# Layer 1 of a two-layer diffusion trunk on one core: inputs of the recurrences projected first, values projected per head and transposed

## The chip, the cores and the metric

The kernel runs on one core of a Trainium2 chip. Its time is the device time of one execution in microseconds; the time of a kernel is the median of several executions. Engines are named as in the profile: PE (TensorE, matrix products), DVE (VectorE), ACT (ScalarE), POOL (GpSimd), SP (SyncE, whose queue issues nearly all transfers here).

## The reference, cut to what matters

Two layers over 1024 latent and 256 context tokens of 1024 channels; each is a mixer and a SwiGLU FFN. Layer 1's mixer is a bidirectional chunked GLA of four heads beside a bidirectional RG-LRU of 512 channels:

```python
def project(h):
    q, k, v, g, lr, zg, zx = jnp.split(h @ w_in, ODD_SPLITS, axis=-1)
    ...
    logit = jnp.einsum('btnr,nrk->btnk', lr, gate_w) + gate_b
    log_a = jax.nn.log_sigmoid(logit) / GLA_GATE_NORM          # per head and direction
    xr = centred_conv(zx, conv_w, conv_b)                       # four taps
    return q, k, v, log_a, g, zg, xr
...
for d in range(2):                                              # forward and backward
    oc, S_ctx = gla_chunked(f(qc), f(kc), f(vc), f(lac[:, :, d]), S0)
    ol, _ = gla_chunked(f(ql), f(kl), f(vl), f(lal[:, :, d]), S_ctx)
    ac, uc = rglru_coeffs(f(xrc), wa[d], ba[d], wx[d], bx[d], lam[d])
    hcd = linear_scan(ac, uc, h0)                               # h = a * h + u, token by token
    al, ul = rglru_coeffs(f(xrl), wa[d], ba[d], wx[d], bx[d], lam[d])
    hld = linear_scan(al, ul, hcd[:, -1])
...
y_gla = rms_norm(o_gla, gla_g).reshape(B, T, -1) * jax.nn.silu(g)
y_lru = h_lru * jax.nn.gelu(zg)
return jnp.concatenate([y_gla, y_lru], axis=-1) @ w_out
```

## The kernel before

Tokens lie in three chunks `CH`: 256 of context, 512 and 512 latent. Activations are kept with channels on the partitions. A product of full precision is made from three of reduced precision: weight and activation are each split into a high and a low part, and `mm3` adds high x high, low x high and high x low over 8 slices of the 1024 channels, so one projection of 128 output channels costs 24 products for each token chunk. `wload` brings a weight piece of 128 output channels (512 KB), copies the high part on ACT and subtracts for the low part on POOL.

Layer 1 begins with `kq` of heads 0 to 2 (at the end of `layer0`), then `layer1`: `proj_lr` (the gates' low rank part); then, woven one step against one, `gla_gates` (for each head three products into the one PSUM bank of tag `d`, a log-sigmoid on DVE, ACT and POOL, a store `dz` to HBM) and `proj1v` (values of all four heads for 128 tokens at a time: the tokens are the stationary operand and 512 value columns move, so that tokens come out on the partitions as the GLA wants them; its weights are split by `v1_load`). Then `kq` of head 3, and the list `LO`, which names single-letter steps with a part or head number m:

- x: `proj_zx`, inputs of the RG-LRU, part m of four, stored to HBM as `dzx`;
- z: `proj_zg`, its gelu gate, a chain of DVE and ACT steps from PSUM on tile `gt`, stored as `dzg`;
- l: `lru`, the recurrence of part m: `zx` loaded back, the four-tap convolution `xr` on DVE, twelve gate products `lg`, their tanh on ACT (`tr`, `ti`), then for both directions exponentials, square roots and the scans (`lq`) on ACT, POOL and DVE;
- p: `gla_prep` of head m in three token chunks: loads of `kq` and `dz`, running sums (`pc`) by scans on DVE, exponentials on ACT, products (`pb`, `pk`, `qh`) on POOL and DVE, stores. Every tile of it has one buffer;
- g: `proj_g`, the GLA's output gate (`stg`).

After the list come the GLA's heads: `gla_states` transposes the stored keys (`kt`), and `gla_half` loads `kq`, `V`, `C`, makes differences `D` on POOL, their exponential on ACT, and products `kx`, `qx` on DVE for the intra-chunk matrices.

Projections and `lg` take their PSUM banks in turn from seven (`BANKS`). A scheduler fixes the order of each engine's instructions when the kernel is built; each engine, and SP's queue of transfers, then runs strictly in that order. Tiles in SBUF and banks in PSUM are reused when their last reader is done.

Of the kernel before, what the change touches and what calls it, by code (L numbers as in the profile page):

```python
# [46 lines left out]
ZA, ZB, ZL = 1, 1, 0  # L47
VQ = (0, 2)
# [74 lines left out]

def weave(a, b, na, nb=1, lead=0):

    live = [True, True]

    def step(i, gen, n):
        for _ in range(n):
            if live[i] and next(gen, run) is run:  # L130
                live[i] = False

    step(0, a, lead)
    while any(live):
# [4 lines left out]
class Trunk:
# [1373 lines left out]
    def v1_load(self, pool):  # L1513
        nc, a = self.nc, self.a
        vh = pool.tile([P, KT, 512], F32R, name="v1h")
        vl = pool.tile([P, KT, 512], F32R, name="v1l")
        for q in range(4):
            raw = self.wraw(a["w1v"][q], f"v1_{q}")
            raw = raw.rearrange("p (k c) -> p k c", k=2)
            nc.scalar.activation(vh[:, 2 * q:2 * q + 2], raw, AF.Copy)  # L1520
            (nc.vector if q in VQ else nc.gpsimd).tensor_tensor(vl[:, 2 * q:2 * q + 2], raw, vh[:, 2 * q:2 * q + 2].bitcast(F32), op=ALU.subtract)
        return vh, vl
# [154 lines left out]
    def layer1(self, h, h2x, l1):  # L1677
# [21 lines left out]
        w = self.wload(a["w1"][3], "w1_3")  # L1699
        for ci in range(3):  # L1700
            self.kq_chunk(w, h[ci], 3, ci, pp, "pk", 1)
        for op, m in LO:
            if op == "x":
                self.proj_zx(h, lp, m)
            elif op == "z":
                self.proj_zg(h, lp, m)
            elif op == "g":
                self.proj_g(h, lp, m)
            elif op == "p":
                self.gla_prep(pp, m)  # L1710
            else:
                self.lru(lp, m)
# [209 lines left out]
def prep(i):  # L1922
# [84 lines left out]
```

## Time and profile before

| | us |
|---|---|
| median of 3 executions (3209.05 to 3218.72) | 3209.83 |
| profiled execution, device time | 3204.12 |
| its span from first to last instruction | 3201.9 |
| PE busy, of the span | 2921.8 (91%) |
| DVE busy | 2186.1 (68%) |
| ACT busy | 1266.0 (40%) |
| POOL busy | 1268.2 (40%) |

The profile shows one execution: for each engine which instruction ran when, and for idle time which event ended it. Matrix products are pipelined, so a busy PE is not one at its peak: pace is read from the distance of starts. The clock granted to TensorE is a share of full speed, where 1.00 is 2.4 GHz and 0.50 is 1.2 GHz.

### The profile page before, as it was taken

The numbers are of one execution on the slowest core, as the hardware profiler recorded it, in microseconds if no ns is written. First come the engines' busy times: TensorE is split into PE (matmuls) and PEld (weight loads), VectorE is DVE, ScalarE is ACT, GpSimd is POOL, SyncE is SP. The second block draws the span as 40 slices with busy tenths as digits, with TensorE's granted clock in tenths as the row PEclk, the third lists the DMA queues.
The fourth block names the chain that finished last, engine by engine and source line by source line (L and its number), as shares of the span: only waits on it lengthen the run. The fifth ranks groups of instructions, "written<-read, shape, count | busy, mean of one in ns | idle before, by whom it ended". The sixth has DMA issues, their size and how long they took to land. (4 is left out here: it accounts for less than half of the span.)

```text
span 3201.9 us, 40796 instructions
## 1 busy us (share of the span) xinstructions
PE 2921.8 (91%) x14848; PEld 2380.8 (74%) x14848; DVE 2186.1 (68%) x3700; ACT 1266.0 (40%) x1956; POOL 1268.2 (40%) x745
## 2 busy tenths in 40 slices
PE   7998899988979999999989998866888999999988
PEld 4987677766768888888877777645677777778877
DVE  5598878885686555556688517879867675645487
ACT  4311655653442232324453444463333332333343
POOL 2333423332233233234445224454545444333445
PEclk9999899998989999999999999987999999999998
DMA  6576433315425444447423235465323232233452
GB/s 250 173 239 204 113 90 88 99 31 188 156 81 162 145 152 152 145 151 273 154 83 112 93 105 187 155 204 187 105 87 99 79 100 93 95 104 104 151 177 98
DMA packets 214920, 437.49 MB, mean 137 GB/s; under 512 B 23424, under 2 KB 86656, under 8 KB 214464
## 3 DMA queue, kind: packets, MB, share of 16 engines
q1 hardware_dynamic: 210112, 418.12, 40.2%
q10 hardware_dynamic: 4608, 16.78, 1.7%
q8 instruction: 116, 1.90, 0.2%
q14 instruction: 84, 0.69, 0.1%
HBM read 325.11 MB, written 109.71 MB: 136 GB/s over the span
## 5 line engine op out<-in xcount | busy, mean ns | idle before, releaser
L263 DVE SCALAR_TENSOR_TENSOR adaw<-adaw,cr 128x1024 f32<-128x1024 f32 x96 | 139.2, 1450 | 88.2 <-DMA adaw<-adat 88.1
L758 POOL TENSOR_TENSOR l_fx<-r_fin,h_fx 128x1024 fp32r<-128x1024 f32 x36 | 87.8, 2439 | 266.5 <-ACT h_fx L757 266.5
L758 POOL TENSOR_TENSOR l_fw<-r_fin,h_fw 128x1024 fp32r<-128x1024 f32 x36 | 87.1, 2420 | 167.4 <-ACT h_fw L757 147.6
L537 POOL TENSOR_SCALAR s_d<-s_d,cf_d 128x1280 f32<-128x1280 f32 (+1 forms) x40 | 46.6, 1165 | 255.4 <-DVE nb_d L524 97.2
L517 PE MATMUL ps_d<-kd,q 128*128 128x512 f32 (+1 forms) x416 | 119.9, 392 | 16.1 <-DVE s_d L519 12.4
L519 DVE TENSOR_SCALAR_CACHE_REDUCE s_d<-ps_d 128x512 f32<-128x512 f32 (+1 forms) x208 | 116.8, 581 | 12.9 <-PE ps_d L517 11.9
L870 DVE TENSOR_TENSOR r_fin<-r_fin,r_fin 128x512 f32<-128x512 f32 x36 | 24.9, 691 | 135.8 <-POOL l_fx L758 135.5
L363 PE MATMUL pq<-hhi,h_w 128*128 128x512 f32 (+1 forms) x312 | 113.4, 363 | 2.6 <-DVE yl L434 2.6
L363 PE MATMUL pq<-hlo,h_w 128*128 128x512 f32 (+1 forms) x312 | 111.6, 358 | 0.0
L363 PE MATMUL pq<-hhi,l_w 128*128 128x512 f32 (+1 forms) x312 | 111.5, 357 | 0.0
L530 ACT ACTIVATE s_d<-s_d,nb_d 128x1280 f32<-128x1280 f32 (+1 forms) x80 | 94.6, 1184 | 23.8 <-DVE nb_d L525 21.5
L538 POOL TENSOR_TENSOR s_d<-s_d,s_d 128x1280 f32<-128x1280 f32 (+1 forms) x40 | 99.6, 2491 | 3.3
L1630 PE MATMUL pg<-qx,kx 128*128 128x128 f32 x448 | 70.8, 308 | 32.8 <-DVE qx L1626 30.1
L956 POOL TENSOR_TENSOR bl<-r_b,bh 128x1024 fp32r<-128x1024 f32 (+2 forms) x32 | 65.4, 2052 | 85.0 <-ACT bh L955 82.3
L1630 PEld LDWEIGHTS pg<-qx,kx 128*128 128x128 f32 x448 | 63.3, 216 | 43.4 <-issue 21.1
L431 POOL TENSOR_TENSOR rsh<-rsh,rope 128x512 f32<-128x512 f32 x26 | 40.7, 1567 | 135.4 <-DVE rsh L428 96.3
L517 PEld LDWEIGHTS ps_d<-kd,q 128*128 128x128 f32 x416 | 70.4, 198 | 31.8 <-DVE s_d L519 18.1
L956 POOL TENSOR_TENSOR bl_0t<-r_b0t,bh_0t 128x1024 fp32r<-128x1024 f32 (+1 forms) x24 | 67.4, 2815 | 62.3 <-ACT bh_0t L955 62.3
L363 PE MATMUL pd<-bh,h_fo 128*128 128x512 f32 (+1 forms) x228 | 85.8, 378 | 5.4 <-DVE xz L1012 3.0
L1620 POOL TENSOR_TENSOR D<-C,V 128x256 f32<-128x256 f32 x56 | 49.1, 876 | 103.0 <-DVE qx L1626 91.8
L327 DVE TENSOR_TENSOR nacc<-nacc,nsq 128x512 f32<-128x512 f32 (+1 forms) x77 | 75.9, 989 | 19.1 <-ACT nsq L326 16.9
L1622 ACT ACTIVATE D<-D 128x512 f32<-128x512 f32 x56 | 35.3, 630 | 134.5 <-POOL D L1621 134.5
(629 smaller groups left out, 10447.6 us busy)
## 6 DMA issues: line engine op xcount, KB each, us to landing
r_fin<-fin SPq DMA_DIRECT2D x104, 512.0 KB, 3.6
adaw<-adat SPq DMA_DIRECT2D x64, 512.0 KB, 3.7
q<-dq SPq DMA_DIRECT2D x160, 128.0 KB, 3.0
adaw<-adat ACTq DMA_DIRECT2D x32, 512.0 KB, 4.5
r_wo<-wo SPq DMA_DIRECT2D x32, 512.0 KB, 3.8
w<-fo SPq DMA_DIRECT2D x32, 512.0 KB, 6.8
r_w<-w SPq DMA_DIRECT2D x29, 512.0 KB, 4.1
dbt<-et SPq DMA_DIRECT2D x44, 256.0 KB, 2.4
```

Source lines behind the costliest of these rows:

```text
L263: nc.vector.scalar_tensor_tensor(o, w, 1.0, cs[v], op0=ALU.mult, op1=ALU.mult, accum_out=self.adac[l][:, m, v:v + 1])
L327: nc.vector.tensor_tensor(acc, acc, sq, op=ALU.add)
L363: nc.tensor.matmul(out, w[wi][wsl(k)], x[xi][xsl(k)], start=(first and k == 0 and i == 0), stop=(last and k == nk - 1 and i == 2), skip_gr ...
L517: nc.tensor.matmul(pt[:, 0:kn], q[:, m, ab, j * P:(j + 1) * P], kt[:, m, k0:k0 + kn], start=(ab == 0), stop=(ab == 1))
L519: nc.vector.tensor_scalar(s[m][:, k0:k0 + kn], pt[:, 0:kn], 1.0, None, op0=ALU.mult, op1=ALU.max, accum_out=mx[:, m, c:c + 1])
L530: nc.scalar.activation(s[m][:, 0:nk * P], s[m][:, 0:nk * P], AF.Exp, bias=nb[:, m:m + 1], scale=SC, accum_out=sm[:, m:m + 1])
L537: nc.gpsimd.tensor_scalar(a1, a1, cf, 0.0, op0=ALU.mult, op1=ALU.add)
L538: nc.gpsimd.tensor_tensor(a0, a0, a1, op=ALU.add)
L758: eng.tensor_tensor(lo[:, 0:n], raw[:, 0:n], hi[:, 0:n].bitcast(F32), op=ALU.subtract)
L956: eng.tensor_tensor(lo[:, 0:n], raw, hi[:, 0:n].bitcast(F32), op=ALU.subtract)
L1620: nc.gpsimd.tensor_tensor(w4(d)[:, :, 0], r, w4(v)[:, :, 0], op=ALU.subtract)
L1630: nc.tensor.matmul(pg[:, b], kx[:, b], qx[:, b], start=True, stop=True)
```

## The change

Layer 1's list is cut in two. `LA1` holds the inputs and gates of recurrences 0 and 1, the recurrences themselves and the values of heads 0 and 1, and is woven with the gates; `LO` holds the rest. Values are projected like every other part, with a weight piece per head as the stationary operand and the tokens moving; the result has channels on the partitions, is copied to SBUF by ACT, transposed in blocks of 128 by PE into the bank of tag `d`, copied again and stored. The pieces are new columns 16 to 19 of `w1`. `pz` and `pe` of the gates have one buffer instead of two. `kq` of head 3 becomes step k of the second list.

```diff
-ZA, ZB, ZL = 1, 1, 0
-VQ = (0, 2)
+ZA, ZB, ZL = 2, 1, 0
...
-LO = [(o[0], int(o[1])) for o in "x0 x1 z0 l0 z1 p0 x2 g0 l1 p1 x3 z2 g1 l2 z3 p2 g2 g3 p3 l3".split()]
+ops = lambda text: [(o[0], int(o[1])) for o in text.split()]
+
+LA1 = ops("x0 z0 x1 l0 v0 z1 l1 v1")
+LO = ops("x2 z2 l2 k3 p0 x3 z3 v2 l3 p1 v3 p2 g0 p3 g1 g2 g3")
...
-            z = pool.tile([P, NTOK], F32, tag="pz", bufs=2, name=f"pz{m}")
-            e = pool.tile([P, NTOK], F32, tag="pe", bufs=2, name=f"pe{m}")
+            z = pool.tile([P, NTOK], F32, tag="pz", bufs=1, name=f"pz{m}")
+            e = pool.tile([P, NTOK], F32, tag="pe", bufs=1, name=f"pe{m}")
...
-    def proj1v(self, h, pool, v):
...
-                pv = self.psum(f"pv1_{tt}", BANKS)
-                self.mm3(pv, [x[:, :, j * P:(j + 1) * P] for x in h[ci]], v, KT,
-                         lambda k: (slice(None), k), lambda k: (slice(None), k))
-                st = pool.tile([P, 512], F32, tag="st", bufs=3, name=f"stv{tt}")
-                self.evac(st, pv, tt)
-                nc.sync.dma_start(self.dv[:, tt, :], st)
+    def proj_v(self, h, pool, m):
+
+        nc = self.nc
+        for ci, pt in self.proj(16 + m, h, (0, 1, 2), "pv"):
+            c0, cn = CH[ci]
+            t0, nt = c0 // P, cn // P
+            f = pool.tile([P, 512], F32, tag="st", bufs=4, name=f"vf{m}{ci}")
+            nc.scalar.activation(f[:, 0:cn], pt, AF.Copy)
+            pv = self.psum(f"vt{m}{ci}", "d")
+            for j in range(nt):
+                nc.tensor.transpose(pv[:, j * P:(j + 1) * P], f[:, j * P:(j + 1) * P], self.ident)
+            st = pool.tile([P, 512], F32, tag="st", bufs=4, name=f"stv{m}{ci}")
+            self.evac(st[:, 0:cn], pv[:, 0:cn], ci)
+            nc.sync.dma_start(self.dv[:, t0:t0 + nt, m * P:(m + 1) * P], st[:, 0:cn].rearrange("p (t c) -> p t c", c=P))
...
-            with self.pool("v1") as vp, self.pool("vs") as vs, self.pool("pg") as pp:
-                v = self.v1_load(vp)
-                weave(self.gla_gates(pp), self.proj1v(h, vs, v), ZA, ZB, ZL)
...
+        with self.pool("pg") as pg:
+            weave(self.gla_gates(pg), stages(LA1, None), ZA, ZB, ZL)
         pp = l1.enter_context(self.pool("pp"))
...
+        run(stages(LO, pp))
```

What this makes of the order is shown at three places. First PE at the first recurrence, before: the last product of gate `zg8_2` (part 0's second latent chunk), then the group `lg` (the digits after the part number are direction, gate and first token).

```order
L363 MATMUL zg8_2_17296<-h227_16346,h_w1_8_17260 128x512
L1388 MATMUL lg0000_17349<-xr0_17336,r_lg0_17345 128x256
L1388 MATMUL lg000256_17352<-xr0_17336,r_lg0_17345 128x512
L1388 MATMUL lg000768_17355<-xr0_17336,r_lg0_17345 128x512
L1388 MATMUL lg0010_17358<-xr0_17336,r_lg0_17345 128x256
L1388 MATMUL lg001256_17361<-xr0_17336,r_lg0_17345 128x512
L1388 MATMUL lg001768_17364<-xr0_17336,r_lg0_17345 128x512
L1388 MATMUL lg0100_17379<-xr0_17336,r_lg0_17345 128x256
```

And now: the last product of the inputs of part 1, and gate products `lz` of GLA head 2 inside the group.

```order
L365 MATMUL zx13_2_16863<-h227_16346,h_w1_13_16803 128x512
L1434 MATMUL lz2_0_16893<-lrt_16531,gw_16532 128x256
L1390 MATMUL lg0000_16922<-xr0_16909,r_lg0_16918 128x256
L1390 MATMUL lg000256_16925<-xr0_16909,r_lg0_16918 128x512
L1390 MATMUL lg000768_16928<-xr0_16909,r_lg0_16918 128x512
L1390 MATMUL lg0010_16931<-xr0_16909,r_lg0_16918 128x256
L1390 MATMUL lg001256_16934<-xr0_16909,r_lg0_16918 128x512
L1434 MATMUL lz2_256_16897<-lrt_16531,gw_16532 128x512
L1390 MATMUL lg001768_16937<-xr0_16909,r_lg0_16918 128x512
L1390 MATMUL lg0100_16952<-xr0_16909,r_lg0_16918 128x256
```

The group has moved from behind the gates of part 0 to behind the inputs of part 1, beside the GLA gates. Second the DVE at the end of the last recurrence (part 3, `lq30` forward and `lq31` backward), before:

```order
L1491 SCALAR_TENSOR_TENSOR stg31_18430<-stg31_18430,g7_1_18405 128x512
L1491 SCALAR_TENSOR_TENSOR stg32_18459<-stg32_18459,g7_2_18434 128x512
L1399 SCALAR_TENSOR_TENSOR ti30_18563<-ti30_18563,xr3_18551 128x1280
L1397 SCALAR_TENSOR_TENSOR lq30_18583<-lq30_18583,tr30_18562 128x1280
L1400 TENSOR_TENSOR ti30_18563<-ti30_18563,lq30_18583 128x1280
L1402 SCALAR_TENSOR_TENSOR lq30_18583<-av30_18582,ti30_18563 128x1280
L1397 SCALAR_TENSOR_TENSOR lq31_18613<-lq31_18613,tr31_18592 128x1280
L1626 TENSOR_TENSOR kx0_18667<-kq00_18742,D000_18762 64x4x64
L1626 TENSOR_TENSOR kx0_18667<-qk00_18744,D000_18762 64x4x64
L1399 SCALAR_TENSOR_TENSOR ti31_18593<-ti31_18593,xr3_18551 128x1280
```

And now, where `stv` are the copies of transposed values, `pc`, `pz` belong to `gla_prep` (two digits: head and chunk) and `stg` to the output gates:

```order
L1402 TENSOR_TENSOR ti31_18117<-ti31_18117,lq31_18137 128x1280
L1407 SCALAR_TENSOR_TENSOR lq31_18137<-av31_18136,ti31_18117 128x256
L1408 SCALAR_TENSOR_TENSOR lq31_18137<-av31_18136,lq31_18137,ti31_18117 128x1024
L1482 TENSOR_TENSOR pc12_18207<-pqk12_18202,pf12_18208 64x512
L1483 TENSOR_TENSOR pc12_18207<-pkq12_18201,pb12_18219 64x512
L1411 SCALAR_TENSOR_TENSOR lq31_18137<-lq31_18137,gl3_18073 128x1024
L1309 COPY stv30_18266<-vt30_18263 128x256
L1462 SCALAR_TENSOR_TENSOR pc20_18345<-ones_71,pz20_18344 128x128 x2
L1465 TENSOR_TENSOR pz20_18344<-pc20_18345,pz20_18344 64x256
L1309 COPY stv32_18336<-vt32_18331 128x512
```

Before, the recurrence ends among the GLA's first steps (`kx`, `qx`); now it ends ahead of the values of head 3 and of `gla_prep` of heads 2 and 3. Third SP's queue of transfers at the hand-over to the GLA's first head (names ending in 00 and `kh0`, `vs0`, `lvm` are its loads), before:

```order
L1477 DMA dkt3_16497<-pk32_18536 128x512
L1492 DMA dsg2_16471<-stg22_18395 128x512
L1482 DMA dqh3_16493<-pc32_18520 128x512
L1372 DMA gl3_18549<-dzg3_16506 128x1024
L189 DMA r_wo1131_19460<-wo1 128x1024
L1492 DMA dsg3_16472<-stg31_18430 128x512
L1556 DMA kh0_18661<-dkt0_16494 128x1280
L1492 DMA dsg3_16472<-stg32_18459 128x512
L1558 DMA vs0_18663<-dv_16481 128x10x128
L1543 DMA lvm_18665<-lvm 128x896
L1596 DMA kq00_18742<-dkq0_16105 128x512
```

And now:

```order
L1459 DMA pz32_18539<-dz3_16604 128x512
L1494 DMA dsg3_16472<-stg32_18751 128x512
L1534 DMA lvm_18795<-lvm 128x896
L1587 DMA kq00_18872<-dkq0_16105 128x512
L1467 DMA dc3_16485<-pc32_18540 128x512
L1468 DMA dvv3_16489<-pz32_18539 128x512
L1592 DMA qk00_18874<-dkq0_16105 64x512
L1479 DMA dkt3_16497<-pk32_18556 128x512
L1593 DMA qk00_18874<-dkq0_16105 64x512
L1484 DMA dqh3_16493<-pc32_18540 128x512
L1587 DMA V00_18877<-dvv0_16486 128x512
L1587 DMA C00_18879<-dc0_16482 128x512
```

The GLA's loads of `V` and `C` stood behind the last store of `gla_prep` by way of output gates; now they stand right behind it, and `lvm` and `kq00` wait ahead of it for the end of the projections.

## Rows read from the trace of the kernel before

**Rows 1.** Busy us (instructions) by stretch: PE, PEld, DVE, ACT, POOL, clock, DMA, GB/s
```profile
1840.00:1908.00 68.00, 68.00 (x274) 48.84 (x274) 11.21 (x17) 28.76 (x32) 18.36 (x7) 1.00 0.33 115
1908.00:2090.00 182.00, 159.64 (x664) 119.92 (x663) 124.66 (x131) 89.11 (x132) 81.39 (x57) 0.92 0.52 167
2090.00:2161.00 71.00, 46.62 (x173) 33.45 (x172) 57.23 (x48) 40.89 (x54) 40.26 (x29) 0.84 0.62 197
2161.00:2320.00 159.00, 119.24 (x658) 98.89 (x657) 142.53 (x269) 56.81 (x86) 84.50 (x81) 0.85 0.46 147
```

**Rows 2.** Timeline of DVE: start, us, engine, line, out<-in, size, xcount [idle before <-releaser]
```profile
2010.52 1.21 DVE L1409 SCALAR_TENSOR_TENSOR lq<-lq,gl 128x1024 f32<-128x1024 f32 x1
...
2160.90 0.84 DVE L1626 TENSOR_TENSOR kx<-kq,D 64x256 f32<-64x256 f32 x1
...
2162.23 1.49 DVE L1399 SCALAR_TENSOR_TENSOR ti<-ti,xr 128x1280 f32<-128x1280 f32 x1
...
2172.45 1.22 DVE L1409 SCALAR_TENSOR_TENSOR lq<-lq,gl 128x1024 f32<-128x1024 f32 x1 [1.66 <-POOL lq L1408]
```

**Rows 3.** Timeline of PE: recurrence groups lg, with projections between
```profile
1960.16 3.60 PE L1388 MATMUL lg<-xr,r_lg 128*128 128x256 f32 x10
...
1973.93 6.72 PE L1388 MATMUL lg<-xr,r_lg 128*128 128x256 f32 x12 [5.65 <-DVE gt L1359]
...
1980.09 0.79 PE L363 MATMUL zg<-h,h_w 128*128 128x512 f32 x1
...
2062.34 0.39 PE L363 MATMUL g<-h,h_w 128*128 128x512 f32 x1
...
2073.23 0.59 PE L1388 MATMUL lg<-xr,r_lg 128*128 128x256 f32 x2
...
2074.70 2.64 PE L1388 MATMUL lg<-xr,r_lg 128*128 128x512 f32 x6 [0.88 <-DVE xr L1378]
...
2090.23 0.79 PE L363 MATMUL zg<-h,h_w 128*128 128x512 f32 x1
...
2137.11 1.19 PE L1388 MATMUL lg<-xr,r_lg 128*128 128x256 f32 x2 [13.65 <-issue]
```

**Rows 4.** Timeline of PE: eight transposes of the GLA
```profile
2277.59 1.04 PE L1566 MATMUL kt<-ident,kh 128*128 128x128 f32 x8
```

**Rows 5.** Timeline of DVE: zx of part 0 copied, and back from HBM
```profile
1941.14 0.67 DVE L1307 COPY stx<-zx 128x512 f32<-128x512 f32 x1
...
1950.54 0.82 DVE L1376 TENSOR_SCALAR xr<-zx,lp 128x1024 f32<-128x1024 f32 x1 [2.88 <-DMA zx<-dzx]
1951.39 3.93 DVE L1378 SCALAR_TENSOR_TENSOR xr<-zx,lp,xr 128x1024 f32<-128x1024 f32 x3
```

**Rows 6.** Timeline of DVE: scans of gla_prep, and two zg steps between
```profile
1960.74 1.85 DVE L1460 TENSOR_TENSOR_SCAN pc<-ones,pz 128x128 f32<-128x128 f32 x4 [3.59 <-DMA pz<-dz]
...
1963.82 1.13 DVE L1356 TENSOR_SCALAR gt<-gt 128x512 f32<-128x512 f32 x1 [0.43 <-ACT gt L1355]
...
1973.19 0.69 DVE L1359 SCALAR_TENSOR_TENSOR gt<-gt,zg 128x512 f32<-128x512 f32 x1 [0.70 <-ACT gt L1358]
...
1978.04 2.75 DVE L1460 TENSOR_TENSOR_SCAN pc<-ones,pz 128x128 f32<-128x128 f32 x4 [0.68 <-DMA pz<-dz]
...
2020.25 0.74 DVE L1460 TENSOR_TENSOR_SCAN pc<-ones,pz 128x128 f32<-128x128 f32 x2 [2.22 <-DMA dqh<-pc]
...
2025.04 1.37 DVE L1460 TENSOR_TENSOR_SCAN pc<-ones,pz 128x128 f32<-128x128 f32 x4 [1.85 <-DMA pz<-dz]
...
2044.12 1.37 DVE L1460 TENSOR_TENSOR_SCAN pc<-ones,pz 128x128 f32<-128x128 f32 x4 [1.09 <-DMA pz<-dz]
```

**Rows 7.** Timelines of DVE (first row) and POOL, the same stretch
```profile
2002.41 7.58 DVE L1378 SCALAR_TENSOR_TENSOR xr<-zx,lp,xr 128x256 f32<-128x256 f32 x1
...
2002.62 2.38 POOL L199 TENSOR_TENSOR l_w<-r_w,h_w 128x1024 fp32r<-128x1024 f32 x1
...
2007.32 2.39 POOL L199 TENSOR_TENSOR l_w<-r_w,h_w 128x1024 fp32r<-128x1024 f32 x1
```

More of the change, by code (lines that the diff above doesn't have):

```diff
@@ L1511, in proj_lr @@
             nc.vector.tensor_copy(self.lrt[:, c0:c0 + cn], pt[0:64, 0:cn])
[L1513 to L1522, printed above, removed]
-    def proj1v(self, h, pool, v):
-        nc = self.nc
-        tt = 0
-        for ci, (c0, cn) in enumerate(CH):
-            for j in range(cn // P):
-                pv = self.psum(f"pv1_{tt}", BANKS)
-                self.mm3(pv, [x[:, :, j * P:(j + 1) * P] for x in h[ci]], v, KT,
-                         lambda k: (slice(None), k), lambda k: (slice(None), k))
-                st = pool.tile([P, 512], F32, tag="st", bufs=3, name=f"stv{tt}")
-                self.evac(st, pv, tt)
-                nc.sync.dma_start(self.dv[:, tt, :], st)
-                tt += 1
-                yield
+    def proj_v(self, h, pool, m):
+        nc = self.nc
+        for ci, pt in self.proj(16 + m, h, (0, 1, 2), "pv"):
[9 more added lines that the diff above has]
+            nc.sync.dma_start(self.dv[:, t0:t0 + nt, m * P:(m + 1) * P], st[:, 0:cn].rearrange("p (t c) -> p t c", c=P))
     def gla_setup(self, pool):
@@ L1690, in layer1, with stages @@
         self.lru_setup(lx.enter_context(self.pool("lr", "right")))
-        with self.pool("lq", "right") as pool:
-            self.lrt = pool.tile([64, NTOK], F32, name="lrt")
-            self.proj_lr(h, pool)
-            with self.pool("v1") as vp, self.pool("vs") as vs, self.pool("pg") as pp:
-                v = self.v1_load(vp)
-                weave(self.gla_gates(pp), self.proj1v(h, vs, v), ZA, ZB, ZL)
-        lp = lx.enter_context(self.pool("l1", "right"))
-        pp = l1.enter_context(self.pool("pp"))
[L1699 to L1712, printed above, removed]
+        pool = lx.enter_context(self.pool("lq", "right"))
+        self.lrt = pool.tile([64, NTOK], F32, name="lrt")
+        self.proj_lr(h, pool)
+        lp = lx.enter_context(self.pool("l1", "right"))
+        def stages(todo, pp):
+            for op, m in todo:
+                if op == "x":
+                    self.proj_zx(h, lp, m)
+                elif op == "z":
+                    self.proj_zg(h, lp, m)
+                elif op == "g":
+                    self.proj_g(h, lp, m)
+                elif op == "v":
+                    self.proj_v(h, lp, m)
+                elif op == "p":
+                    self.gla_prep(pp, m)
+                elif op == "k":
+                    w = self.wload(a["w1"][m], f"w1_{m}")
+                    for ci in range(3):
+                        self.kq_chunk(w, h[ci], m, ci, pp, "pk", 1)
+                else:
+                    self.lru(lp, m)
+                yield
+        with self.pool("pg") as pg:
+            weave(self.gla_gates(pg), stages(LA1, None), ZA, ZB, ZL)
+        pp = l1.enter_context(self.pool("pp"))
+        run(stages(LO, pp))
         l1.close()
@@ L1947, in prep @@
     cols = np.concatenate([np.concatenate([256 + np.arange(64) + 64 * h, np.arange(64) + 64 * h]) for h in range(4)]
-                          + [1024 + np.arange(512), 1568 + np.arange(512), 2080 + np.arange(512)])
+                          + [1024 + np.arange(512), 1568 + np.arange(512), 2080 + np.arange(512), 512 + np.arange(512)])
     o["w1"] = pieces(w[:, cols])
-    o["w1v"] = np.ascontiguousarray(w[:, 512:1024].reshape(4, 2, P, 512).transpose(0, 2, 1, 3).reshape(4, P, 1024))
     o["w1lr"] = np.ascontiguousarray(w[:, 1536:1568].reshape(KT, P, 32).transpose(1, 0, 2))
```

## The prediction, made before the changed kernel had run

> **What bounds the kernel now.** I read the stage from the last normalised tokens of layer 1 (1840 us) to the first step of the chunked GLA (the DVE's first `kx` product, 2160.9 us) [rows 1, 2]; what lies behind it keeps its order on every engine but for a few rows at the first head. The table of busy times shows two halves [rows 1]. Up to 1908 TensorE is busy for all of its 68 us while the DVE has 11.2 us of work: gates and values are projected and nothing else can run. From 1908 on the DVE has 124.7 us in 182 and TensorE stands for 22; from 2090 to 2161 it stands for 24 of 71.
>
> TensorE's own timeline shows where [rows 3]. A recurrence begins with twelve gate products `lg`. At full clock a 512-column one takes 0.88 us (six instructions, two to a product, in 2.64) and I take 0.45 for a 256-column one, so a group is 8 x 0.88 + 4 x 0.45 = 8.8 us. The first group takes 19.9 us (1960.16 to 1980.09), the third 17.0 (2073.23 to 2090.23); the second I put at the first's. The bank that a product needs is still held there by a gate chunk (5.65 us in one go, released by the DVE's step on `gt`), and that step stands behind `gla_prep`. Ahead of the fourth, projections end near 2123 (six chunks of 5.44 behind 2090.23), then it waits 13.65 for its input, and nothing is left to project beside it. Waits: 11.1 + 11.1 + 8.2 in the groups and, from 2123 to 2160.9 less the group's 8.8, some 29 at the end: 60 us of 321. The change attacks these 60.
>
> **The change part by part.** *Products.* The values are the same columns with operands exchanged: 240 products of 512 columns become, per head, 24 products each of 256, 512 and 512. At 48 products in 10.89 us (2062.34 to 2073.23) a 512 one costs 0.227, a half one 0.12; a head is 13.8 and four are 55 us, as before. Added are 40 transposes: eight took 1.04 us [rows 4], so 5.2 us. The page "TensorE: Matmul & The Clock Gate" of the Trainium skill (Part 4) speaks against this: it gives about 275 ns for one in a kernel, and says that they don't keep the clock up. By that the 40 would cost 11 us and the forecast would be some 6 us later; the row has them at half that, and they come in twos and fours between projections.
>
> *Evacuation and weights.* Ten copies of 0.7 us become twelve plus twelve, half of them on ScalarE, which is busy for 28.8 of the first 68 us: no cost while it isn't behind. Of four weight splits two leave the DVE for POOL: it runs four of 2.4 us where it ran two. They hide beside projections that run for 13.8 us each.
>
> *TensorE up to the last recurrence.* With the new order, ahead of recurrence 3 stand four `zx` (55), four `zg` (43.6), three heads of values (41.4), `kq3` (13.8), three recurrence groups (26.4), the gates (68 us less 54.5 of values leaves 13.5, in which `kq3` starts: 11) and 30 transposes (3.9): 195 us, so 2035 if nothing waits. I add these waits. `pz` and `pe` have one buffer now: the next head's gates wait for the previous store; 3 us (0 to 6). The value transposes share one PSUM bank with the gates; `vt0` of head 0 comes some 32 us behind the first product of recurrence 0 (the group, two gates, a head of values, a third more than one chunk of `zg`), and the bank is free only after that recurrence has let the DVE go: 6 (0 to 17). Head 1: 2 (0 to 5). `zx` of part 2 goes to HBM and back with only the 10.9 us of `zg10` to cover it; its like took 8.7 us from the end of the copy to the first DVE step and 4.8 more to the last one [rows 5], and with the copy's 0.7 that is 14.2: 4 (0 to 8). Slow clock after these waits: 3 (in the stretch with most waits the granted clock is 0.84 [rows 1]). Together 18, so recurrence 3 starts near **2053** (2035 to 2070). The groups themselves should run near 9 us: what stands before them now is `zx` and values, whose banks are emptied by plain copies.
>
> *The last recurrence.* `vt31` needs the bank from the copy of `vt30`, which stands on the DVE behind the last step of recurrence 3, and `gla_prep` of heads 2 and 3 stands behind that copy. Recurrence 0 took 51.6 us from its first product to its last step (1960.16 to 2011.73 [rows 2, 3]). TensorE's waits in the group are 11.1 of them, which leaves 40; DVE steps of `gla_prep` and of `zg` between them, most of which stand elsewhere now, take a few more off: **37** (27 to 45). TensorE arrives at `vt31` after 8.8 + 13.8 + 4, so it waits some 10 us there, hidden from the end only if the next chain is longer.
>
> *The tail.* Six chunks of `gla_prep` then run one behind the other, for each tile has one buffer: a chunk's scan waits for the load of `pz`, that for the stores of the chunk before. Scan to scan took 4.8 us behind a short chunk and 17.3 and 19.1 behind a long one [rows 6]. Of the 17.3, six DVE steps of `zg` (the first and the last shown, 4.3 us in all) were in between, and I take 13. The chunks are 2c0, 2c1, 2c2, 3c0, 3c1, 3c2: steps of 5, 13, 13, 5, 13, and then 18 from the last scan to the first `kx`: on SP's queue the GLA's loads of `V` and `C` stand behind the store of that chunk's `qh`, where the next chunk's load of `pz` stands otherwise (13), and POOL's two differences and ScalarE's exponential follow (5, an estimate). That is **67** (50 to 83). TensorE beside it has 43.6 us of `g` and is no longer last.
>
> *The sum.* 2053 + 37 + 67 = 2157, against 2160.9: 4 us. Recurrence 3 also leaves the GLA's start: five of its DVE steps, 7.3 us, stood behind the first `kx` (the first and the last in [rows 2]), in a stretch where the DVE is busy for 142.5 of 159 us [rows 1]. So 11 us. The profiled execution is 3201.9 of span in 3204.1 us, hence 3193; the median shown, 3209.8, is 5.7 above it, and 3209.8 - 11 = **3199** is the forecast.
>
> **The rivals.** *TensorE sets the end.* If ScalarE, POOL and SP keep the six chunks within the 43.6 us of `g` and the transposes don't wait, projections end at 2053 + 8.8 + 13.8 + 43.6 + 1.3 = 2120.5, the GLA starts 14 us later, and the gain is 26 + 7 = 33: 3177. For it: in the tail the DVE has little else. Against: one buffer for each tile.
>
> *The recurrences stay as long as they were.* POOL's and DVE's work keep each other waiting: one 256-column DVE step took 7.58 us while POOL ran three operations of 2.4 us back to back, the first starting 0.2 us after it [rows 7]. If that holds recurrences 0 and 3 at 45 us and more, `vt0` and the tail come 8 us later each: 2157 + 16 = 2173, 12 later, less 7.3: 5 us lost, 3215. The page "SBUF — State Buffer" of the Trainium skill (two separate sides) has the rule: DVE operations with two inputs in SBUF and POOL's lock each other out for a whole instruction. By that rule the trace agrees, and POOL's two more splits fall where it would bite. Against it: the recurrences now run beside projections, with the six chunks elsewhere.
>
> *Slower: the chunks at their measured pace.* With 18 us instead of 13 for each of the three long steps, and the 83 of the upper end rather than 67, the first `kx` comes at 2173 and the loss is 12 - 7 = 5; with SP's queue, where stores of `g` that wait for TensorE stand between the loads of `pz`, 3 us more for each long step: 2182, a loss of 21 - 7 = 14, 3224. It decides from where the chain of six is 78 us and longer.
>
> **How the numbers follow.** About 0.3% (9.6 us) is what a measurement of this kernel can tell from no change. Forecast 0.42 (gains of 4 to 20); TensorE sets the end 0.22; recurrences as long as before 0.20; chunks at their measured pace 0.16. Faster by over 0.3%: the second case and some three quarters of the first, 0.52. Slower by over 0.3%: the last, 0.16. The rest, 0.32, is within it. The range that leaves out a tenth at either end: 3177 (TensorE sets the end) to 3218 (between the last two).
>
> **What would show it.** In the profile after: the `lg` groups of recurrences 0 to 2 at 9 to 12 us; TensorE's idle time named by the copies of `vt` and by `xr`, not by `gt` or `stg`; `vt31` waiting some 10 us for the DVE; scans of `pc` 12 to 14 us apart in the tail, with TensorE done some 25 us before the first `kx`; that `kx` near 2157; no step of a recurrence behind it. I am wrong if the first recurrence is still on the DVE 45 us after its first product, if the GLA's first loads don't wait for `qh` of head 3, or if the time gained is given back behind 2320, where TensorE is busy nearly throughout.

## The result, and the profile after

The changed kernel took 3244.24 us (median of 4 executions, 3238.88 to 3250.99) against 3209.44 of the kernel before: a ratio of 1.0101, 95% interval 1.0082 to 1.0121. That is some 32 us slower, where 11 faster were forecast, and outside the range (3177 to 3218). The profiled execution is 3245.6 us of span.

The busy times of the same four stretches as in [rows 1], columns as there:

```profile
1840.00:1908.00 68.00, 65.14 (x277) 46.80 (x276) 28.02 (x32) 37.22 (x43) 17.95 (x7) 0.97 0.28 95
1908.00:2090.00 182.00, 153.50 (x671) 116.83 (x670) 114.35 (x113) 97.53 (x130) 70.66 (x44) 0.92 0.43 137
2090.00:2161.00 71.00, 58.99 (x251) 47.84 (x249) 44.74 (x44) 26.94 (x44) 32.50 (x21) 0.93 0.47 155
2161.00:2320.00 159.00, 99.56 (x542) 84.47 (x543) 115.88 (x233) 49.00 (x78) 77.47 (x82) 0.75 0.59 184
```

The first stretch has done what was meant: the DVE now has 28.0 us of work in it, where it had 11.2. But TensorE has lost its full first stretch, and in the last one it is busy for 99.6 us of 159, at a granted clock of 0.75 instead of 0.85. TensorE's waits up to the GLA's first product, grouped by what waited for what (us in total, times, longest), before:

```profile
PE lg L1388 <- issue: 13.6, 1, 13.6
PE lg L1388 <- DVE gt L1359: 13.2, 3, 5.7
PE kt L1566 <- ACT ti L1389: 9.5, 1, 9.5
PE lg L1388 <- DVE stg L1491: 8.2, 2, 5.0
PE lg L1388 <- DVE xr L1378: 2.2, 2, 1.3
```

and after:

```profile
PE kt L1557 <- DMA kh<-dkt: 34.5, 1, 34.5
PE vt L1525 <- ACT vf L1522: 12.7, 4, 4.0
PE vt L1525 <- ACT pe L1436: 8.3, 1, 8.3
PE lg L1390 <- DVE xr L1380: 7.7, 1, 7.7
PE vt L1525 <- DVE stv L1309: 6.4, 1, 6.4
PE lz L1434 <- ACT pe L1436: 2.9, 2, 1.6
```

The change removed what it was aimed at: `gt` and `stg` no longer appear, and nor does the wait ahead of the last recurrence (the 13.6 called issue). In their place stand 27.4 us at the transposes `vt` (12.7, 8.3 and 6.4), 7.7 for an input `xr`, and 34.5 for the load of the first stored keys `kh`, with the projections done since 2158.6. Idle rows sum to 46.7 us before and 75.5 after. The first GLA product came 320.5 us behind the first gate product before (1839.93 to 2160.41), and comes 352.6 behind it now (1840.50 to 2193.07): 32 us more, of which 29 are in the idle rows.

Where the 34.5 us come from is read on the DVE: the last step of recurrence 3, then the scan that begins each chunk of `gla_prep`, then the first `kx` (it answers to [rows 2, 6]):

```profile
2114.31 1.23 DVE L1411 SCALAR_TENSOR_TENSOR lq<-lq,gl 128x1024 f32<-128x1024 f32 x1
...
2117.24 0.74 DVE L1462 TENSOR_TENSOR_SCAN pc<-ones,pz 128x128 f32<-128x128 f32 x2 [1.37 <-issue]
...
2127.61 3.53 DVE L1462 TENSOR_TENSOR_SCAN pc<-ones,pz 128x128 f32<-128x128 f32 x4 [0.32 <-DMA pz<-dz]
...
2143.89 1.37 DVE L1462 TENSOR_TENSOR_SCAN pc<-ones,pz 128x128 f32<-128x128 f32 x4 [5.72 <-DMA pz<-dz]
...
2155.39 0.74 DVE L1462 TENSOR_TENSOR_SCAN pc<-ones,pz 128x128 f32<-128x128 f32 x2 [3.79 <-DMA pz<-dz]
...
2160.93 1.88 DVE L1462 TENSOR_TENSOR_SCAN pc<-ones,pz 128x128 f32<-128x128 f32 x4 [3.62 <-DMA pz<-dz]
...
2176.94 1.37 DVE L1462 TENSOR_TENSOR_SCAN pc<-ones,pz 128x128 f32<-128x128 f32 x4 [6.44 <-DMA pz<-dz]
...
2192.13 0.75 DVE L1617 TENSOR_TENSOR kx<-kq,D 64x256 f32<-64x256 f32 x1 [8.36 <-ACT D L1613]
```

Six chunks stand one behind the other: 10.4, 16.3, 11.5, 5.5 and 16.0 us from scan to scan, then 15.2 from the last scan to `kx`, which waits for `D`. TensorE's wait for `kh` ends at the same place, and not because its keys are late: it loads those of head 0, whose last store had left at 2055.10. On SP's queue the load stands behind the stores of the last chunk, that of head 3:

```profile
2184.16 0.54 SPq L1484 DMA_DIRECT2D dqh<-pc  x1
...
2185.26 0.43 SPq L1587 DMA_DIRECT2D C<-dc  x1
...
2186.22 0.42 SPq L1547 DMA_DIRECT2D kh<-dkt  x1
```

Whether only the order of the queue holds the load there, or also the space of its tile, is open: no run moved it alone.

### The profile page after: what moved, and what is told of

The parts are those of the page before. It is cut to its first block, busy times and chain, and to the rows that moved or that the text cites. A ratio compares the mean times of both kernels' runs of the same rounds, so it can differ in the third digit from the quotient of the medians.

```text
span 3245.6 us, 41003 instructions
## 1 busy us (share of the span) xinstructions
PE 2932.7 (90%) x14936; PEld 2395.3 (74%) x14936; DVE 2177.5 (67%) x3701; ACT 1271.6 (39%) x1967; POOL 1266.3 (39%) x747
## 5 line engine op out<-in xcount | busy, mean ns | idle before, releaser
L539 POOL TENSOR_SCALAR s_d<-s_d,cf_d 128x1280 f32<-128x1280 f32 (+1 forms) x40 | 46.7, 1169 | 255.1 <-DVE nb_d L526 97.1
L519 PE MATMUL ps_d<-kd,q 128*128 128x512 f32 (+1 forms) x416 | 118.0, 386 | 17.5 <-DVE s_d L521 13.6
L521 DVE TENSOR_SCALAR_CACHE_REDUCE s_d<-ps_d 128x512 f32<-128x512 f32 (+1 forms) x208 | 116.5, 581 | 14.0 <-PE ps_d L519 13.2
L201 POOL TENSOR_TENSOR l_w<-r_w,h_w 128x1024 fp32r<-128x1024 f32 x33 | 86.6, 2627 | 94.8 <-ACT h_w L200 87.9
L519 PEld LDWEIGHTS ps_d<-kd,q 128*128 128x128 f32 x416 | 69.1, 195 | 32.7 <-DVE s_d L521 18.8
L201 POOL TENSOR_TENSOR l_wo<-r_wo,h_wo 128x1024 fp32r<-128x1024 f32 x24 | 59.0, 2459 | 77.2 <-ACT h_wo L200 77.0
```

What stands on the lines that cost most here:

```text
L201: eng.tensor_tensor(lo, raw, hi.bitcast(F32), op=ALU.subtract)
L519: nc.tensor.matmul(pt[:, 0:kn], q[:, m, ab, j * P:(j + 1) * P], kt[:, m, k0:k0 + kn], start=(ab == 0), stop=(ab == 1))
L521: nc.vector.tensor_scalar(s[m][:, k0:k0 + kn], pt[:, 0:kn], 1.0, None, op0=ALU.mult, op1=ALU.max, accum_out=mx[:, m, c:c + 1])
L539: nc.gpsimd.tensor_scalar(a1, a1, cf, 0.0, op0=ALU.mult, op1=ALU.add)
```

## The experiments

In all of them the first number is the ratio to the kernel before, timed beside it on the same chip. Letters mark the five questions.

**A. The transposes.** Their bank, and all of them.

```diff
-            pv = self.psum(f"vt{m}{ci}", "d")
+            pv = self.psum(f"vt{m}{ci}", BANKS)
```

> Changed kernel, with the value transposes in the seven projection banks instead of the one bank of the gates. Two theories of the 35 us lost. T1: the twelve gla_prep chunks set the end; ten of them run from 2041 on, at some 13 us each, with recurrence 3 among them, so TensorE's waits cost little. T2: TensorE's new waits at the value transposes (8.3 + 12.7 + 6.4 us and the slow clock after them) bring recurrence 3 25 us late, and that is what is lost. T1 expects 0 to 6 us off the changed kernel's 3244 (ratio to before 1.009 to 1.011) with the first kx at 2186 to 2192; T2 expects 14 us off for the two bank waits (ratio near 1.006), the first kx near 2177.

Measured: 1.0105 (1.0088 to 1.0122), no gain, as T1 had it. The bank was not what held them up: another one only moved the waits (24.3 us for ACT's copy `vf` and 11.5 at the gates `lz`).

```diff
-            pv = self.psum(f"vt{m}{ci}", "d")
-            for j in range(nt):
-                nc.tensor.transpose(pv[...], f[...], self.ident)
-            st = pool.tile([P, 512], F32, tag="st", bufs=4, name=f"stv{m}{ci}")
-            self.evac(st[:, 0:cn], pv[:, 0:cn], ci)
-            nc.sync.dma_start(self.dv[...], st[...])
+            nc.sync.dma_start(self.dv[...], f[...])
```

> Changed kernel without the 40 value transposes and their second copies: the projection's copy is stored as it is, so the values stand in the wrong places. T1 expects recurrence 3 to start some 25 us earlier (near 2055) and the first kx to move by less than 12 of these, to 2180 or later (ratio 1.007 to 1.010). T2 expects all 25 us and more at the end: the first kx near 2165, ratio 1.002 or less.

Measured: 1.0068 (1.0052 to 1.0084), 11 us gained, at the edge of what T1 named and far from T2. Recurrence 3 began at 2063.9, 14 us earlier and not 25, and the GLA's first product at 2186.7, 6 us earlier. TensorE's largest waits in it:

```profile
PE kt L1552 <- DMA kh<-dkt: 44.9, 1, 44.9
PE lz L1434 <- ACT pe L1436: 10.8, 3, 8.2
```

Its projections ended at 2141.9 instead of 2158.6, and then it waited 44.9 us for the load of `kh` instead of 34.5.

**B. The place of gla_prep.** Earlier in the list, two buffers, and both. (R2, which two texts name, is the theory that recurrences first is itself the fault; it is tested under C.)

```diff
-LO = ops("x2 z2 l2 k3 p0 x3 z3 v2 l3 p1 v3 p2 g0 p3 g1 g2 g3")
+LO = ops("x2 z2 k3 p0 l2 p1 x3 z3 v2 p2 l3 v3 p3 g0 g1 g2 g3")
```

> Changed kernel with the second list in another order: gla_prep of heads 0 to 2 ahead of the recurrences 2, 3 and the values that they stood behind (x2 z2 k3 p0 l2 p1 x3 z3 v2 p2 l3 v3 p3 g0 g1 g2 g3). TensorE's work and its transposes stay. T1 expects the first kx 15 to 30 us earlier (2162 to 2177), ratio 1.001 to 1.006. T2 expects no gain, since recurrence 3 comes no earlier and gla_prep only takes the DVE ahead of it: ratio 1.010 to 1.014.

Measured: 1.0048 (1.0033 to 1.0063), as T1 had it. TensorE's first GLA product came at 2175.9 instead of 2193.1; but the first `kx`, which T1 put at 2162 to 2177, came at 2186.5.

```diff
             def tl(tag, bufs=1):
+                bufs = 2 if tag in ('pz', 'pc') else 1
```

> Changed kernel with two buffers for gla_prep's pz and pc, so that a chunk's load and scan need not wait for the stores of the chunk before. T1 expects the five steps between the scans of the tail to fall from 12 us on average to 8 to 10, and the first kx 10 to 20 us earlier (2172 to 2182), ratio 1.004 to 1.008. T2 expects less than 5 us, ratio 1.009 to 1.011.

Measured: 1.0045 (1.003 to 1.006), as T1 had it; first GLA product at 2177.1, but first `kx` at 2187.7 and not by 2182. T1 was right on both ratios and wrong on both times of `kx`. The two together:

> Changed kernel with both: gla_prep earlier in the list (as in x3_pfirst) and two buffers for pz and pc (as in x4_prep2). In its order one chunk is left behind the last recurrence. T1 expects the gains to add in good part: TensorE's first kt at 2160 to 2168 where each alone gave 2176 and 2177, ratio 0.998 to 1.002. T2 and R2 expect no more than either alone: ratio 1.004 or more.

Measured: 1.0077 (1.006 to 1.0094), no better than either: from the first gate product to the GLA's first it took 335.5 us, where the two alone had 336.4 and 337.3. The wait for `kh` has shrunk to 2.1 us, and TensorE comes late by itself:

```profile
PE vt L1526 <- ACT vf L1523: 31.0, 5, 19.0
```

A chunk that comes early stands ahead of something that TensorE waits for. One transpose now waits 19.0 us for its copy `vf` (at 2077.84 on ACT), and ACT had stood still for a chunk's scan, with the gelu steps and `vf` queued behind:

```profile
2059.63 0.58 ACT L1357 ACTIVATE gt<-zg 128x512 f32<-128x512 f32 x1
2072.03 0.63 ACT L1465 ACTIVATE pz<-pc 64x512 f32<-64x512 f32 x1 [11.82 <-DVE pc L1463]
```

And with the transposes gone as well:

> x7_pfirst_prep2 without the value transposes and their second copies (the values stand in the wrong places, as in x2_notrans). So far either cure left the other bound: without transposes TensorE was done at 2142 and waited 45 us for gla_prep; with gla_prep early it waited 2 us there, but it came late itself (19 us in one wait at a transpose). T4: the two bounds lie near each other, and both have to go. T4 expects TensorE's first kt at 2148 to 2166 and a ratio of 0.995 to 1.001. If there is a third bound (recurrences one behind the other, TensorE waiting for their inputs), the ratio is 1.003 or more.

Measured: 1.0037 (1.0019 to 1.0055): some 21 of the 32 us are gone, but T4 fell. There is a third bound, the input of the last recurrence:

```profile
PE lg L1390 <- DVE xr L1380: 28.2, 1, 28.2
```

On the DVE the long steps on `xr3` (2083.54 to 2093.0) stand behind two scans of `gla_prep` that wait 5.6 and 1.9 us for their loads. Next, the gates first, so that `gla_prep` can begin earlier, and then one list with the chunks beside the recurrences:

```diff
-ZA, ZB, ZL = 2, 1, 0
+ZA, ZB, ZL = 2, 1, 12
```

> Changed kernel with all twelve gate steps ahead of the first list instead of woven into it; both lists as they are. The earlier runs leave this theory, T3: recurrences (some 40 us each) and chunks of gla_prep (some 13 each) add up, less what runs side by side; the kernel before has most chunks between the steps of recurrences (201 us from the first recurrence's first product to the first kx), the changed one has them behind (302, about 4 x 40 + 11 x 13). Here gla_prep can start near 1915 instead of 1955, and in the order two chunks come beside the first recurrence, but six are still behind the last. T3 expects a small gain at most: ratio 1.006 to 1.011. If the late start of gla_prep were the fault (its tiles take the gates' space), the ratio would be 1.002 or less.

Measured: 1.0104 (1.0089 to 1.0119), as T3 had it: the first scan at 1922 instead of 1959, six chunks still behind the last recurrence, 32.4 us of waiting for `kh`.

> Changed kernel with the gates first and one list in which each gla_prep stands right behind the recurrence before it (x0 z0 x1 l0 v0 p0 z1 l1 v1 x2 z2 p1 l2 k3 x3 z3 p2 l3 v2 p3 v3 g0 g1 g2 g3): in the order two or three chunks lie beside each recurrence and one behind the last. The values stay per head and transposed. T3 expects the loss gone: TensorE's first kt at 2150 to 2168, ratio 0.996 to 1.002. T2 (TensorE's waits at the transposes decide) expects 1.006 or more.

Measured: 1.0082 (1.0065 to 1.0098); a miss. The same with the two buffers, and then with more lead for the inputs:

> x10_onelist with two buffers for gla_prep's pz and pc: in its order no chunk is left behind the last recurrence. T3 expects it 0 to 10 us faster than x10_onelist, until TensorE's own work and waits set the end: ratio 0.994 to 1.001.

Measured: 1.0089 (1.0074 to 1.0104).

> As x11_onelist_prep2, with gla_prep ahead of its recurrence, the inputs of each recurrence one step further ahead of it and the last recurrence ahead of the last values (x0 z0 x1 p0 l0 v0 z1 x2 p1 l1 v1 z2 x3 k3 p2 l2 v2 z3 p3 l3 v3 g0 to g3). T3 expects TensorE's wait for the inputs of recurrences 2 and 3 (7.7 us in the changed kernel) under 3 us and the end no later than x11: ratio 0.992 to 1.000. T2 expects it no better than x11, since the transposes are the same.

Measured: 1.006 (1.0041 to 1.0079). All three missed in the same way. The wait for `kh` is gone (about 1 us in each), and the wait for `xr` has taken its place; in x10_onelist:

```profile
PE lg L1390 <- DVE xr L1380: 30.8, 4, 11.3
PE vt L1525 <- ACT vf L1522: 9.4, 6, 3.5
```

So T3's sum, as if the side engines' work could be laid beside TensorE's at will, was too simple: it is a question of who stands ahead of whom in each engine's queue.

**C. Either half of the change alone.** The new order with the old values, and the new values with the old order.

```diff
-LO = ... "x0 x1 z0 l0 z1 p0 x2 g0 l1 p1 x3 z2 g1 l2 z3 p2 g2 g3 p3 l3".split()]
+LO = ... "x0 z0 x1 l0 z1 l1 x2 z2 l2 p0 x3 z3 l3 p1 p2 g0 p3 g1 g2 g3".split()]
```

> Kernel before with its old values and gates (projected together first) and only the list in the new manner: inputs and gates of each recurrence right ahead of it, the recurrences first, gla_prep and g behind (x0 z0 x1 l0 z1 l1 x2 z2 l2 p0 x3 z3 l3 p1 p2 g0 p3 g1 g2 g3). No transposes. In its order one chunk of gla_prep stands behind the last recurrence, where the changed kernel has six, since the gates are done by 1908 and gla_prep begins there. T1 (the chunks of gla_prep set the end) expects the loss gone: ratio to before 0.994 to 1.000. A rival, R2: recurrences first is itself the fault (recurrence 3 on the DVE ahead of the last chunks, as in the changed kernel): ratio 1.005 to 1.010.

Measured: 1.0092 (1.0072 to 1.0111): R2, not T1. There is no transpose of values in it, and it loses nearly as much as the whole change. TensorE waits for the inputs of recurrences:

```profile
PE lg L1388 <- DVE xr L1378: 29.5, 3, 14.7
PE kt L1566 <- DMA kh<-dkt: 12.2, 1, 12.2
PE lg L1388 <- issue: 10.7, 1, 10.7
```

```diff
-LA1 = ops("x0 z0 x1 l0 v0 z1 l1 v1")
-LO = ops("x2 z2 l2 k3 p0 x3 z3 v2 l3 p1 v3 p2 g0 p3 g1 g2 g3")
+LA1 = ops("v0 v1 v2 v3")
+LO = ops("k3 x0 x1 z0 l0 z1 p0 x2 g0 l1 p1 x3 z2 g1 l2 z3 p2 g2 g3 p3 l3")
```

> Changed kernel with the new values (per head, transposed) and the old order: values of the four heads beside the gates, then kq3, then the list of before. T1 expects a loss no larger than the transposes and the waits beside the gates, with the chunks of gla_prep where they were: ratio 1.000 to 1.004. R2 expects the same; T2 (TensorE's waits at the transposes) expects most of the 35 us here too: ratio 1.006 to 1.010.

Measured: 1.0129 (1.0111 to 1.0148), the slowest of all, beyond every outcome named. Here the last gates were stored at 1949 instead of 1920, and the first load of `pz` left at 1954 instead of 1907. With the gates first, and then without transposes too:

> x6_oldorder (new values, old order) with all gate steps first. In x6_oldorder the last gates were stored at 1949 and gla_prep's first load left at 1952, where in the kernel before it left by 1908. In the order here four chunks stand ahead of the first recurrence, as in the kernel before (five). If the late gates are what cost x6_oldorder its 41 us: ratio 1.000 to 1.005. If it is the transposes and their waits (T2): 1.009 or more, as x6_oldorder had 1.013.

Measured: 1.0094 (1.0058 to 1.013): the second outcome, by a wide interval.

> x14_oldorder_gatesfirst without the value transposes and their second copies (values in the wrong places). In x14 values, gates and kq3 took 113 us of TensorE where the kernel before has 82, and the end came as much later. If the transposes (the bank they share with the gates, the copy they wait for, the slow clock behind it) are the cause, the stretch falls to 82 to 88 us and the ratio to 0.998 to 1.004. If it is the gates ahead of the values, the stretch stays above 100 us and the ratio above 1.006.

Measured: 1.0043 (1.003 to 1.0056). The stretch of values, gates and `kq` of head 3 tells it: one row each of x14_oldorder_gatesfirst, x16_oldorder_notrans and the kernel before, columns as in [rows 1]:

```profile
1842.30:1955.30 113.00, 96.61 (x425) 72.00 (x425) 16.69 (x30) 43.42 (x56) 21.93 (x9) 0.89 0.25 79
```

```profile
1842.10:1939.70 97.60, 88.59 (x385) 66.60 (x385) 13.23 (x22) 40.54 (x51) 21.91 (x9) 0.93 0.27 84
```

```profile
1839.90:1921.70 81.80, 81.80 (x337) 59.84 (x337) 13.94 (x24) 37.74 (x43) 22.04 (x12) 1.00 0.32 109
```

113.0, 97.6 and 81.8 us, which lies between the two outcomes named. Taking the transposes and their second copies out saves 15 us of the difference. The other 16 go with the gates in a row: 9.0 us are TensorE's waits `lz <- pe`, behind their one buffer, and the granted clock is 0.93 instead of 1.00. This part is read, not tested.

**D. What gla_prep costs either kernel.** Its arithmetic taken out of both (the same edit: each chunk loads `kq` and `dz` and stores them as they are).

> Changed kernel with gla_prep's arithmetic left out: each chunk only loads and stores its tiles. This leaves TensorE's own waits and the recurrences. If gla_prep behind the recurrences is the last bound of the changed kernel, the 34.5 us of TensorE's idle time before the first kt fall under 16 (a load) and projections end at 2140 to 2158: kt at 2150 to 2170, ratio 0.996 to 1.002. If the recurrences alone hold TensorE as long (T2 and the waits for xr), projections end no earlier and the ratio is 1.003 or more.

Measured: 0.9943 (0.9929 to 0.9958), first GLA product at 2145.6: faster than the first outcome named.

> Kernel before with gla_prep's arithmetic left out in the same way. In the kernel before the chunks lie between the steps of the recurrences; if they cost it little there, the first kt comes at 2145 to 2160 and the ratio is 0.994 to 1.000. If they stretch its recurrences (51.6 us for the first, 38 in the changed kernel without a chunk beside it), each gets 10 us shorter, kt comes at 2120 to 2140 and the ratio is 0.986 to 0.993: then gla_prep costs both kernels the same, and only its place in the order differs.

Measured: 0.9864 (0.9847 to 0.988), first GLA product at 2119.7; the second outcome. TensorE's waits up to there, first of x17_after_noprep, then of x18_before_noprep:

```profile
PE vt L1509 <- ACT pe L1436: 8.4, 1, 8.4
PE lg L1390 <- DVE xr L1380: 7.6, 1, 7.6
PE vt L1509 <- ACT vf L1506: 6.2, 4, 2.2
PE lz L1434 <- ACT pe L1436: 2.8, 2, 1.6
```

```profile
PE kt L1550 <- ACT ti L1389: 12.4, 1, 12.4
PE lg L1388 <- DVE stg L1475: 2.2, 1, 2.2
PE lg L1388 <- DVE gt L1359: 1.8, 1, 1.8
```

`gla_prep` costs the changed kernel 1.58% (51 us) and the kernel before 1.36% (44 us): it costs the new order 7 us more than the old one, with some 9 us of uncertainty (from the three intervals). The other 25 remain when it is gone (0.9943 against 0.9864). In this pair of profiles the GLA's first product comes 302.2 and 277.3 us behind the first gate product. Of these 25 us, 12.8 are idle rows (30.4 against 17.6, the smaller ones included): in the upper list transposes that wait for ACT, gates that wait for one buffer, the round trip of `zx`. TensorE's busy time makes the rest (271.8 against 259.8 us), for the transposes themselves and, read, not tested, the slower clock behind the waits. One more thing is in this pair. In x17_after_noprep the output gates end the list, and on SP's queue the GLA's loads of `kq`, `V` and `C` stand behind the last store of `stg` (2145.85): the first `kx` comes at 2158.72, 14 us behind the projections. In x18_before_noprep it comes at 2118.72. What the place of the output gates costs the changed kernel was not tested by itself. The lower list shows that the old order, left to itself, has almost no wait inside its groups: the waits for `gt` and `stg` that the change set out to remove were `gla_prep`'s own steps, ahead of `gt` on the DVE, and they go with it (13.2 and 8.2 us to 1.8 and 2.2).

**E. A version that beats both.** The kernel before with the two buffers alone, and with `g3` moved behind the last recurrence as well.

> Kernel before with two buffers for gla_prep's pz and pc and nothing else. In its order all chunks of gla_prep stand ahead of the third recurrence's steps. T1 expects little or a gain, since in the kernel before the end is set by the last recurrence and the chunks only lie between its steps: ratio 0.994 to 1.001. If two buffers alone were what x4 gained, whatever the order, it would be 0.994 (the same 18 us).

Measured: 0.9981 (0.9966 to 0.9995), first `kx` at 2149.99: some 6 us faster than the kernel before and 38 than the changed one. All its chunks lie ahead of the long steps of recurrence 2, as the order said.

```diff
-... "x0 x1 z0 l0 z1 p0 x2 g0 l1 p1 x3 z2 g1 l2 z3 p2 g2 g3 p3 l3".split()]
+... "x0 x1 z0 l0 z1 p0 x2 g0 l1 p1 x3 z2 g1 l2 z3 p2 g2 p3 l3 g3".split()]
```

> x8_before_prep2 with the last output gate g3 behind the last recurrence instead of ahead of gla_prep of head 3 (end of the list: g2 p3 l3 g3). In x8 TensorE waits 11.3 us at the first kt for the last recurrence's tanh. If recurrence 3 can start earlier by the 10.9 us of g3: ratio to before 0.993 to 0.998 (x8 had 0.998). If its input xr sets its start, g3 only moves behind it and nothing is gained: 0.997 to 1.000.

Measured: 1.005 (1.003 to 1.0071), slower than both outcomes named. Recurrence 3 started no earlier (2127.4 and 2130.4, in a stage that began 2.7 us earlier), as the second outcome had it; and `g3` behind it delays the GLA: its first `kx` comes at 2171.84, 22 us later than without the move.

## Why the prediction was wrong, point by point

**TensorE up to the last recurrence: the step that failed.** The first `kx` came 35 us behind the forecast 2157: 25 of them are lost here, 1 in the last recurrence, 9 in the tail. The work was sized well. But recurrence 3 began 237.5 us behind the first gate product (1840.50 to 2078.01), where 195 of work and 18 of waits were forecast. Idle rows in between sum to 31.4, and some 9 went at the slower clock behind them, where 3 were taken (an estimate, from each busy stretch and its granted clock: 0.69 in 2058.97 to 2067.57). The waits that the prediction put there were the right ones and too short: `vt0` 8.3 where it said 6; the round trip of `zx` of part 2 8.3 with some 2 of slow clock behind it, where it said 4 (0 to 8). The trip itself was as forecast; but the copy that begins it stood on the DVE behind the steps of recurrence 1 and of `gla_prep`, and ended 7.6 us after its product.

The prediction gave nothing to the transposes of head 2, and 7.6 us of idle time came there, with 4 of slow clock. Its sentence "no cost while it isn't behind" of the copies on ACT is the one that broke: ACT is busy for 97.5 of 182 us (the second row above) and still behind, since its instructions run in the order of the program. ACT around the first of these waits (idle time in brackets):

```profile
2052.07 0.58 ACT L1357 ACTIVATE gt<-zg 128x512 f32<-128x512 f32 x1
2056.58 0.63 ACT L1360 ACTIVATE gt<-gt 128x512 f32<-128x512 f32 x1 [3.94 <-DVE gt L1359]
2057.12 0.58 ACT L1357 ACTIVATE gt<-zg 128x512 f32<-128x512 f32 x1
2057.60 1.05 ACT L200 ACTIVATE h_w<-r_w 128x1024 fp32r<-128x1024 f32 x1
2058.54 0.37 ACT L1522 ACTIVATE vf<-pv 128x256 f32<-128x256 f32 x1
```

The copy `vf` could have begun near 2054.7, when the product of its chunk ended. It stands behind two gelu steps on `gt` and a weight copy, and the first of these waits 3.94 us for the DVE. The DVE at that time:

```profile
2052.24 1.68 DVE L1483 TENSOR_TENSOR pc<-pkq,pb 64x512 f32<-64x512 f32 x1
2053.95 1.27 DVE L1378 TENSOR_SCALAR xr<-zx,lp 128x256 f32<-128x256 f32 x1
2055.14 0.41 DVE L1358 TENSOR_SCALAR gt<-gt 128x512 f32<-128x512 f32 x1
2055.48 0.47 DVE L1380 SCALAR_TENSOR_TENSOR xr<-zx,lp,xr 128x256 f32<-128x256 f32 x1
2055.87 0.68 DVE L1359 TENSOR_TENSOR gt<-gt,zg 128x512 f32<-128x512 f32 x1
```

It is at `gla_prep`'s products, then at `xr`, and only then at `gt`. TensorE waits for ACT, ACT for the DVE, and the DVE is at work that TensorE needs later. The same chain, ACT waiting for the DVE, stands behind the waits of 8.3 and 4.0 (with this one, 15.9 of the 27.4 us at `vt`).

**Products and transposes.** Right. TensorE's row for four of them:

```profile
1962.92 0.60 PE L1525 MATMUL vt<-ident,vf 128*128 128x128 f32 x4
```

The projection goes on 0.36 us later, at 1963.28. The page "TensorE: Matmul & The Clock Gate" of the Trainium skill (Part 4) has about 275 ns for one; here the measurement decides, at some 0.1 us. What made them dear is another thing: three runs without them and their second copies, against the same kernels with them, gained 11 us (x2_notrans), 16 (x16_oldorder_notrans against x14_oldorder_gatesfirst) and 13 (x13_notrans_pfirst_prep2 against x7_pfirst_prep2), each uncertain by 8 to 12, for 5 us of instructions.

**The last recurrence.** Right: 37 forecast, 37.9 from its first product to the copy of `vt30` (2078.01 to 2115.87), but partly by luck: the prediction put most steps of `gla_prep` elsewhere, and 13 us of them lie on the DVE in this stretch. One of these, a product that takes 0.69 us elsewhere, took 6.30 at 2107.25 while POOL ran three operations back to back, and ended 0.5 us behind the last. The page "SBUF — State Buffer" of the Trainium skill (two separate sides) has the rule: of a DVE operation with two inputs in SBUF and a POOL operation that reads SBUF, the one that comes second is blocked while the other's instruction lasts. The trace agrees, and here the block lasted through more than one instruction. The groups of recurrences 0 and 1 ran in 10.0 and 11.6 us with the gates between them; that of recurrence 2 took 18.9 for its `xr`. Recurrences 0 to 2 took 39, 43 and 43 us where they had taken 52 to 55, so the rival in which they stay as long did not come.

**The tail.** Undersized: 76.3 us (2115.87 to 2192.13) where 67 were taken and 50 to 83 allowed. The three steps put at 13 took 16.3, 11.5 and 16.0; the two put at 5 took 10.4 and 5.5. The last, put at 18, took 15.2: 13.3 up to POOL's first `D` (2190.24), where 13 were taken, and 1.9 from there, where 5 stood as an estimate that no run had shown. This is the fourth case's mechanism near its bound of 78.

**Recurrence 3 out of the GLA's start.** It did come: 7 us were forecast, and the delay against the kernel before fell from 32.7 us at the first `kt` to 21.1 at the first product of the output projection `pq` (2184.12 and 2205.19). But it was given back, as the prediction's last sign of being wrong has it, and early: the eight transposes of [rows 4] start at 2309.13 now, 31.5 us later than before, with a granted clock of 0.81 from `pq` up to there instead of 0.88. Behind the stretch shown here, the same work on TensorE, first before, then after, the delay stood at 39 us.

```profile
2413.40:2453.80 40.40, 36.21 (x197) 29.57 (x197) 30.23 (x52) 11.93 (x18) 15.33 (x15) 1.00 0.32 98
```

```profile
2450.30:2493.10 42.80, 38.73 (x198) 31.41 (x198) 30.30 (x52) 11.89 (x18) 15.50 (x15) 0.93 0.29 93
```

The granted clock is 0.93 instead of 1.00. Why it stays lower so long after the hand-over is open; nothing was tried on it. (This pair of profiles ends 43.7 us apart, the medians 34.8, and the kernel before alone varies by 12 us, so what came behind the 32 may be scatter.)

**The rivals.** Each of the four cases let one chain set the end. The runs show at least three bounds near each other (TensorE with its waits, the chunks, the inputs of the recurrences): whichever was eased, in x2_notrans, x3_pfirst, x4_prep2, x7_pfirst_prep2 and x13_notrans_pfirst_prep2, the first `kx` came 344 to 349 us behind the first gate product, where the changed kernel has 352 and the kernel before 321. They share the queues of DVE, ACT and POOL, which run in order, so that moving one moves the others. The case in which the inputs come first and TensorE then waits for other copies was not among them. What the prediction would have needed is to ask of each new wait on TensorE what stands ahead of its releaser on that engine, and what that waits for.

So the cause is shown in part. With the transposes out, the chunks earlier and two buffers (x13_notrans_pfirst_prep2), some 21 of the 32 us are gone, and 12 stay. The transposes were taken out only beside `gla_prep`, so their share of the 25 us that remain without it is not measured. The round trip of `zx` (some 10 us with the slow clock), the gates' single buffers and the place of the output gates are read, not shown; none was undone by itself in the changed kernel.

## What to carry to other kernels

When a step is split so that TensorE must wait for a copy of its own result, price the copy by what stands ahead of it in its engine's queue, not by its length or by that engine's busy share. When TensorE waits inside a stage, take the suspected side work out altogether, in both kernels: the pair says how much of a loss belongs to the order and how much to that work. A second buffer for a chain of small steps can give more than an order built around them: here 6 us gained against 32 lost.
